# Weight blocks of 4 KB per partition and scan tables laid out by chunk and group, in a hybrid SSD and attention encoder

## The chip, the core and the metric

The kernel runs on one core of one Trainium2 chip. The time is device microseconds of one launch, as a median over runs. The core's engines run beside each other, each in its own order: TensorE (PE) for matrix products, VectorE (DVE), ScalarE (ACT) and GpSimd (POOL) for the rest, SyncE (SP), which here issues nearly all DMA transfers, and 16 DMA engines that carry them out.

## The reference

One layer over 512 tokens of width 1024, in float32. What is computed:

```
h    = rmsnorm(x) ;  z, xBC, dt, q, k, v, gates = split(h @ w_in)
y_s  = gated_rmsnorm(scan_forward(xBC, dt) + scan_backward(xBC, dt) + x*d_skip, z) @ w_ssd_out
y_a  = window_attention(q, k, v, sink, rel_bias) @ w_attn_out
x    = x + rmsnorm((sigmoid(g_s) * y_s + sigmoid(g_a) * y_a) @ w_o)
x    = x + rmsnorm(relu(rmsnorm(x) @ w_mlp_in)**2 @ w_mlp_out)
```

The scan works in 4 chunks of 128 tokens, in both directions, for 8 groups of 4 heads. Within a chunk the decay between tokens l and s is exp(cs[l] − cs[s]), where cs is the cumulative sum of dt·a over the chunk:

```
cb     = einsum('bclgn,bcsgn->bcgls', c, b)
y_diag = einsum('bcgls,bcgrls,bcsgrp->bclgrp', cb, decay, xdt)
y_off  = einsum('bclgn,bcgrpn,bcgrl->bclgrp', c, prev, exp(a_cs))
```

## The kernel before, in words

**Products.** Each product with a weight runs over blocks of 128 output columns and 1024 input channels. `cm` (L551) makes one "quantum" of each: its block is a tile wr of 128 partitions × 1024 floats (8 pieces of 128 channels), loaded by one DMA of 512 KB (`chunk_raw`, L478). A float32 product is made of three passes on rounded parts: ACT casts the block to wh (L498), POOL subtracts to wl (L502), in four pieces, and `mm3` (L429, with the matmul itself on L423) multiplies wh and wl with the activations' two parts into a bank pp. The activations' parts are made by `split` (L440 ACT for the rounded part, L441 DVE for the rest). In DRAM w_in, w_attn_out, w_ssd_out and w_mlp_in lie row by row, so that a block's partition collects 8 runs of 128 floats, 512 bytes each.

**The scan.** For a group g the conv of the products x, B and C runs on DVE (`conv`, L982 to L986, with L992 and L993 for the silu; the tiles are called u, B, C). `dt_math` makes cs once and writes it and its exp to the DRAM tables csT and csE, 64 rows (direction, group, head) of 512 tokens. For each chunk of each group, `load` (L1129, L1135) fetches rf and rb, the rows of 4 heads copied to all 128 partitions, forward and backward, and E, the exp for two pairs of heads, one head on each half of the partitions. `prep` makes of them, on POOL (L1148), ACT (L1150 to L1155) and DVE (L1145, L1151, L1156, L1157), the masked decay matrix m; PE multiplies m with x. `outs` adds the part from the states, weighed with E (L1185, L1186, L1190, L1191). `rms` (L1198 to L1219) then makes the group's norm: squares summed on POOL (ssq), a matmul with ones (its operand's two parts are called sh and sl), a row of 512 sums written to DRAM (rrow), read back as a column (rcol), raised to −1/2 on POOL (L416, L418), written to DRAM (L1219) and read as a row copied to all partitions (rstd, L408). `finish` multiplies it into the outputs yT on DVE (L1229), four operations in a row.

**Attention** works on heads in between: scores (KH, Q), softmax (P, with L915 to L924), the transposes of P (L427) copied out as pT by ACT or DVE (L935).

**Order.** All is emitted quantum by quantum, and then `chain` (L522) hands a stretch of instructions to a Planner, which simulates the engines with its own costs (L233, among them bytes and a fixed time for a DMA) and due times (L266), chooses each engine's order and fixes it by dependencies. SP's order, and so the place of each DMA among the others, is chosen in the same way. A DMA on SP also waits for the one eight places before it on the queue to land.

Of the kernel before, what the change touches and what calls it, by code (L numbers as in the profile page):

```python
# [65 lines left out]
def packed(given):  # L66

    rows = lambda n: given[n].reshape(-1, 128)
    xt, wv = given["x"][0, :256].T.reshape(8, 128, 256), np.concatenate(
        [given["w_in"][0][:, c:c + n].reshape(8, 128, n) for c, n in ((C_V, 256), (C_DT, 64))], axis=2)  # L70
    pieces = lambda a, cuts: np.concatenate([a[k0:k1].transpose(1, 0, 2).reshape(-1) for k0, k1 in cuts])
    cv = np.concatenate([rows(n) for n in ("conv_w", "conv_b", "b_gate", "ssd_norm", "pre_mlp_norm")]).T
    row = np.concatenate([given[n].reshape(-1) for n in ("dt_bias", "a_log", "attn_sink", "d_skip")])
    bucket, far = buckets()
    bias = np.ascontiguousarray(given["rel_bias_table"][bucket].T)
    bias[:, far] = NEG
    first = np.concatenate([rows("pre_mix_norm").T, xt[0]], axis=1)
    return {"cv": np.ascontiguousarray(cv), "row": row, "bias": bias,
            "xt": np.concatenate([first.reshape(-1), pieces(xt, X_CHUNKS[1:])]), "wv": pieces(wv, V_CHUNKS)}


# [283 lines left out]
class Trunk:  # L365
    def __init__(self, ctx, tc, ins, out, dbg=None):
        self.tc, self.nc, self.out = tc, tc.nc, out
        self.__dict__.update({"d_" + k: v for k, v in ins.items()})
        self.d_w_in = ins["w_in"][0]
# [417 lines left out]
    def dt_math(self):  # L787
# [41 lines left out]
        def rows():  # L829
            px = self.bank("ps")  # L830
            for c in range(4):
                self.tr(px[:64, c * 128:(c + 1) * 128], self.cs[:, c, :])
            csr, cse = get("csr"), get("cse")
            nc.vector.tensor_copy(csr[:64], px[:64])
            nc.scalar.activation(cse[:64], px[:64], AF.Exp)
            self.csT = self.dp.tile([64, 512], F32, name="csT")
            self.csE = self.dp.tile([64, 512], F32, name="csE")
            nc.sync.dma_start(self.csT, csr[:64])
            nc.sync.dma_start(self.csE, cse[:64])
            put(csr, cse)  # L840
            self.show("dt", self.dt)
            self.show("cs", self.cs)
# [5 lines left out]
    def kv_quanta(self):  # L848
        nc = self.nc
        get = self.slots.get  # L850
        self.KH, self.KL = [], []

        def k_done(ps):
            for j in range(2):
                a = slice(j * 64, j * 64 + 64)
                b = slice(64 - j * 64, 128 - j * 64)
                KH, KL = get("KH", dtype=F32R), get("KL", dtype=F32R)
                nc.scalar.copy(KH[a], ps[a])
                nc.vector.tensor_tensor(KL[a], ps[a], KH[a].bitcast(F32), op=ALU.subtract)
# [6 lines left out]
        return [self.cm(self.d_w_in, C_K + 128 * i, hh, k_done) for i in range(2)]  # L866

    def backward(self, ap):

# [2 lines left out]
    def q_quantum(self, i):  # L872

        nc = self.nc

        blocks = lambda ap: ap.rearrange("p (n t) -> p n t", t=128)

        def done(ps):
            for u in range(2):
                a = slice(u * 64, u * 64 + 64)  # L880
                b = slice(64 - u * 64, 128 - u * 64)
                q = self.slots.get("Q", dtype=F32R)
                self.Q[2 * i + u] = q
# [4 lines left out]
        return self.cm(self.d_w_in, C_Q + 128 * i, lambda: self.h, done)  # L888

    def attn_bias(self, h):  # L890
        bt = self.bt[h] = self.slots.get("bt", (128, 384))
# [68 lines left out]
    def gate_quantum(self, m, dst):  # L960
# [5 lines left out]
        return self.cm(self.d_w_in, C_GS + m * 128, lambda: self.h, done)  # L966

    def attn_out_quantum(self, m):
        def done(ps):
# [3 lines left out]
                for hi, lo in self.at_:  # L973
                    self.slots.put(hi, lo)

        return self.cm(self.d_w_attn_out[0], m * 128, lambda: self.at_, done)


    def conv(self, u, ps, b):
# [16 lines left out]
    def ssd_quanta(self, g):  # L996
# [48 lines left out]
        def z_done(i):  # L1045
# [9 lines left out]
            return done  # L1055

        hh = lambda: self.h
        x, rest = [self.cm(self.d_w_in, C_X + 256 * g + 128 * i, hh, x_done(i)) for i in range(2)], [
            self.cm(self.d_w_in, C_B + 128 * g, hh, bc_done("B", 16 + g)),
            self.cm(self.d_w_in, C_C + 128 * g, hh, bc_done("C", 24 + g)),  # L1060
        ]
        z = [self.cm(self.d_w_in, C_Z + 256 * g + 128 * i, hh, z_done(i)) for i in range(2)]
        pool = {"x": x, "B": rest[:1], "C": rest[1:], "z": z}
        return [pool[k].pop(0) for k in ORDER]

    def ssd_steps(self, g):
# [57 lines left out]
        def load(c):  # L1124
            def run():
                ch[c]["r"] = get("rf"), get("rb")
                for d, r in enumerate(ch[c]["r"]):
                    base = self.csT[32 * d + 4 * g:32 * d + 4 * g + 4, c * 128:(c + 1) * 128]
                    nc.sync.dma_start(v4(r), bass.AP(tensor=base.tensor, offset=base.offset, ap=[[0, 128], [512, 4], [1, 128]]))  # L1129
                ch[c]["E"] = get("E", (128, 2, 2, 128))  # L1130
                for d in dirs[3 - c]:
                    base = self.csE[32 * d + 4 * g:32 * d + 4 * g + 4, c * 128:(c + 1) * 128]
                    for i in range(2):
                        src = bass.AP(tensor=base.tensor, offset=base.offset + i * 512, ap=[[0, 64], [1024, 2], [1, 128]])
                        nc.sync.dma_start(ch[c]["E"][i * 64:(i + 1) * 64, d], src)  # L1135
            return run

        def prep(c):
# [157 lines left out]

    def ssd_out_quanta(self):

        w = self.d_w_ssd_out[0]
        banks = []  # L1300

        def part(k0, k1, c, n):
            return w[k0 * 128:k1 * 128, c:c + n].rearrange("(k p) n -> p k n", p=128), k1 - k0, n, "p"

        def most(parts):
            ps = self.bank("pp")
# [5 lines left out]
        def rest(parts):  # L1312
            wh, wl = parts[0]
            for m, ps in enumerate(banks):
                c = slice(m * 128, (m + 1) * 128)
                for k in (14, 15):
                    self.mm3(ps, (wh[:, k - 14, c], wl[:, k - 14, c]), self.ys[k], False, k == 15)
                self.ssd_out_done(ps, m)

        return [Quantum([part(0, 8, m * 128, 128), part(8, 14, m * 128, 128)], most) for m in range(2)] + [  # L1320
            Quantum([part(14, 16, 0, 256)], rest)] + [
            self.cm(w, m * 128, lambda: self.ys, lambda ps, m=m: self.ssd_out_done(ps, m)) for m in range(2, 8)]

    def load_wo(self, j, k):
# [131 lines left out]
        return 8 * part + n // 2 + 4 * (n % 2)  # L1456

    def up_quantum(self, i):
        return self.cm(self.d_w_mlp_in[0], self.block(i) * 128, lambda: self.h2, lambda ps: self.up_done(ps, i))

    def up_halves(self, n):

        w = self.d_w_mlp_in[0]
        chunks = [(w[:, m * 128:(m + 1) * 128].rearrange("(k p) n -> p k n", p=128), 8, 128, "p")
                  for m in map(self.block, range(n))]
        held, banks = [], []

        def product(m, t2):
# [241 lines left out]
```

## Time and profile before

| | us |
|---|---|
| median of 3 runs | 1084.91 (1084.78 to 1085.91) |
| the profiled execution | 1087.15 |
| its span, first to last instruction | 1085.4 |
| PE busy in it | 1072.1 (99%) |
| DVE, ACT, POOL busy | 742.0, 641.8, 801.2 |
| mean granted PE clock | 0.998 |

The profile comes from one execution of its own, a little above the median. Times of rows are microseconds from the span's start. A row of the timeline gives start, length, engine, line, operation and "out<-in" by tile names (numbers left out), a count where like rows were joined, and in brackets the idle time of the engine before it and what ended that. SPq is SP's issue of a DMA, not its transfer; "us to landing" of a DMA is the time from issue to its data being there. PE matmuls overlap by pipelining.

### The profile page before, as it was taken

What the parts mean: (1) busy time and instruction counts of PE and PEld (TensorE: products, weight loads), DVE (VectorE), ACT (ScalarE), POOL (GpSimd) and SP (SyncE); (2) the same over time, 40 slices, a digit from 0 to 9 for tenths busy, and PEclk for the clock granted to TensorE, in tenths of its full rate; (3) what the DMA queues carried; (4) which work ended last, traced back from release to release, by engine and by line L of the source; (5) the groups of instructions that cost most, each with busy time, mean ns of one, the idle gap of its engine ahead of it and who ended that gap; (6) DMA issues with size and microseconds to landing.
All of it is one profiled execution on the core that took longest, in us unless ns stands there. A gap on an engine that the chain in (4) does not pass through costs nothing. (4 is left out here: it accounts for less than half of the span.)

```text
span 1085.4 us, 16598 instructions
## 1 busy us (share of the span) xinstructions
PE 1072.1 (99%) x5542; PEld 897.3 (83%) x5542; DVE 742.0 (68%) x1281; ACT 641.8 (59%) x1378; POOL 801.2 (74%) x986
## 2 busy tenths in 40 slices
PE   9999999999999999999999999999999999999997
PEld 7888888888888888888878888889888888888885
DVE  5777787787787787787788853435673583584698
ACT  7756786776686767676768632323554544444552
POOL 5846558558568798999999876511688898898994
PEclk9999999999999999999999999999999999999999
DMA  8434424533545636354554464524322422424232
GB/s 273 121 101 121 120 78 123 141 98 95 123 108 130 151 112 157 90 165 120 153 150 135 138 191 118 173 82 155 100 75 59 156 80 76 156 77 148 87 98 78
DMA packets 208181, 133.20 MB, mean 123 GB/s; under 512 B 9560, under 2 KB 190296, under 8 KB 208096
## 3 DMA queue, kind: packets, MB, share of 16 engines
q1 hardware_dynamic: 207808, 131.76, 43.0%
q8 instruction: 43, 0.70, 0.3%
q10 hardware_dynamic: 288, 0.39, 0.1%
q14 instruction: 42, 0.34, 0.1%
HBM read 127.63 MB, written 4.49 MB: 122 GB/s over the span
## 5 line engine op out<-in xcount | busy, mean ns | idle before, releaser
L502 POOL TENSOR_TENSOR wl<-wr,wh 128x256 fp32r<-128x256 f32 (+1 forms) x500 | 423.8, 877 | 137.1 <-ACT wh L498 131.2
L423 PE MATMUL pp<-h,wh 128*128 128x512 f32 (+1 forms) x1712 | 523.4, 387 | 0.0
L423 PEld LDWEIGHTS pp<-h,wh 128*128 128x128 f32 x1712 | 316.3, 188 | 62.3 <-issue 0.7
L423 PE MATMUL pp<-h,wl 128*128 128x512 f32 (+1 forms) x856 | 332.3, 388 | 0.0
L498 ACT CAST wh<-wr 128x1024 fp32r<-128x1024 f32 x131 | 136.4, 1042 | 140.1 <-PE pp L423 123.4
L423 PEld LDWEIGHTS pp<-h,wl 128*128 128x128 f32 x856 | 160.8, 188 | 32.5 <-issue 0.5
L1546 POOL TENSOR_TENSOR wl<-wd,wh 128x256 fp32r<-128x256 f32 x158 | 130.4, 862 | 12.0 <-ACT wh L1543 12.0
L1543 ACT CAST wh<-wd 128x512 fp32r<-128x512 f32 x82 | 47.3, 618 | 32.4 <-PE ps L423 16.2
L423 PE MATMUL ps<-wl,fh 128*128 128x512 f32 x164 | 63.9, 390 | 0.0
L423 PE MATMUL ps<-wh,fl 128*128 128x512 f32 x164 | 63.8, 389 | 0.0
L423 PE MATMUL ps<-wh,fh 128*128 128x512 f32 x164 | 63.8, 389 | 0.0
L1413 DVE SCALAR_TENSOR_TENSOR pp<-pp,r 128x512 f32<-128x512 f32 (+1 forms) x31 | 17.6, 568 | 65.0 <-ACT r L1410 64.9
L1154 ACT ACTIVATE n<-cb,tables 128x128 f32<-128x128 f32 x128 | 49.0, 390 | 16.0 <-DVE cb L1145 15.6
L1150 ACT ACTIVATE rf<-rf,tables 128x128 f32<-128x128 f32 x128 | 42.4, 392 | 14.2 <-DMA rf<-csT 14.2
L986 DVE SCALAR_TENSOR_TENSOR u<-pp,cv,u 128x510 f32<-128x510 f32 (+1 forms) x64 | 47.6, 744 | 4.5 <-ACT u L982 3.3
L423 PE MATMUL pp<-yh,wl 128*128 128x512 f32 x128 | 49.8, 390 | 0.0
L423 PE MATMUL pp<-yh,wh 128*128 128x512 f32 x128 | 49.7, 389 | 0.0
L423 PE MATMUL pp<-yl,wh 128*128 128x512 f32 x128 | 49.6, 389 | 0.0
L1155 ACT ACTIVATE m<-cb,tables 128x128 f32<-128x128 f32 x128 | 48.8, 388 | 0.3 <-DVE cb L1145 0.2
L1190 POOL TENSOR_TENSOR w<-w,E 128x256 f32<-128x256 f32 x48 | 37.9, 802 | 14.3 <-DVE w L1186 13.0
L1084 POOL TENSOR_TENSOR xd<-x,tables 128x256 f32<-128x256 f32 x48 | 33.0, 706 | 16.5 <-ACT x L1009 12.8
L918 ACT ACTIVATE P<-P,mx 128x384 f32<-128x384 f32 (+1 forms) x64 | 35.2, 552 | 15.1 <-DVE mx L915 14.9
(273 smaller groups left out, 2158.1 us busy)
## 6 DMA issues: line engine op xcount, KB each, us to landing
wr<-in_w_in SPq DMA_DIRECT2D x74, 512.0 KB, 4.0
wr<-in_w_mlp_in SPq DMA_DIRECT2D x32, 512.0 KB, 4.2
wd<-in_w_mlp_out SPq DMA_DIRECT2D x64, 256.0 KB, 5.5
rf<-csT SPq DMA_DIRECT2D x32, 256.0 KB, 4.7
rb<-csT SPq DMA_DIRECT2D x32, 256.0 KB, 3.3
wr<-in_w_ssd_out SPq DMA_DIRECT2D x14, 512.0 KB, 4.1
E<-csE SPq DMA_DIRECT2D x96, 64.0 KB, 4.1
x<-in_x SPq DMA_DIRECT2D x16, 256.0 KB, 5.5
```

The costliest lines, as they stand in the source:

```text
L423: self.nc.tensor.matmul(out, lhsT, rhs, start=start, stop=stop, skip_group_check=more)
L498: self.nc.scalar.copy(hi[:, :m], raw)
L502: engines[e].tensor_tensor(lo[:, c], raw[:, c], hi[:, c].bitcast(F32), op=ALU.subtract)
L918: nc.scalar.activation(p[:, :w], p[:, :w], AF.Exp, bias=mx[:, n:n + 1], accum_out=sm[:, n:n + 1])
L986: nc.vector.scalar_tensor_tensor(u[:, a:e], ps[:, a + d:e + d], self.wtap(t, b), u[:, a:e], op0=ALU.mult, op1=ALU.add)
L1084: nc.gpsimd.tensor_tensor(v4(xd[:, d * 256:(d + 1) * 256]), v4(xs(c)), by_dir(self.coef, c)[:, d].unsqueeze(2).to_broadcast([128, 4, 64]), ...
L1150: nc.scalar.activation(v4(rf)[:, h], v4(rf)[:, h], AF.Identity, bias=ncs[:, 0, h:h + 1])
L1154: nc.scalar.activation(v4(n)[:, h], cb[:, 0], AF.Copy, scale=dt[:, 0, h:h + 1])
L1155: nc.scalar.activation(v4(m)[:, h], cb[:, 1], AF.Copy, scale=dt[:, 1, h:h + 1])
L1190: nc.gpsimd.tensor_tensor(wc, wc, E[:, d], op=ALU.add)
L1543: nc.scalar.copy(hi, src)
L1546: (nc.vector if q == 512 else nc.gpsimd).tensor_tensor(lo[:, c], src[:, c], hi[:, c].bitcast(F32), op=ALU.subtract)
```

## The change

The host now lays the four weights out in blocks [column block, group of 8 channel pieces, 128 partitions, 8 pieces, 128 columns]; the columns for dt, which have an array of their own already, are left out of w_in's. So every partition's 8 × 128 floats of a block lie together, 4 KB. The first two column blocks of w_ssd_out are loaded in pieces of 8, 6 and 2 channel pieces as before, the last piece for both in one transfer. The tables csT and csE are laid out by chunk, direction and group (csE also by the half of the partitions), so that the 4 heads of rf or rb are one run of 2 KB instead of 4 of 512 bytes, and the pair of heads of E one run of 1 KB instead of two of 512 bytes. E's two directions, where both are needed, come in one transfer for each half of the partitions. csE is written in two transfers instead of one. Arrays that the kernel no longer reads aren't passed. The lines of the changed kernel stand 4 to 8 further down (L1129 is L1136, L1135 is L1140, L478 is L485, L408 is L415, L423 is L430).

```diff
+    blocks = lambda a: np.ascontiguousarray(a.reshape(-1, 8, 128, a.shape[1] // 128, 128).transpose(3, 0, 2, 1, 4))
+    w_in = given["w_in"][0]
+    mats = {"w_in": np.concatenate([w_in[:, :C_DT], w_in[:, C_Q:]], axis=1)}
+    mats.update({n: given[n][0] for n in ("w_attn_out", "w_ssd_out", "w_mlp_in")})
...
+    @staticmethod
+    def inside(base, offset, *dims):
+        return bass.AP(tensor=base.tensor, offset=base.offset + offset, ap=[list(d) for d in dims])
...
-        nk = w.shape[0] // 128
-        chunks = [(w[k0 * 128:(k0 + 8) * 128, c:c + 128].rearrange("(k p) n -> p k n", p=128), 8, 128, eng)
-                  for k0 in range(0, nk, 8)]
+        nk = w.shape[1] * 8
+        chunks = [(w[c // 128, k0 // 8], 8, 128, eng) for k0 in range(0, nk, 8)]
...
-            nc.sync.dma_start(self.csT, csr[:64])
-            nc.sync.dma_start(self.csE, cse[:64])
+            chunks = lambda a: a.rearrange("p (c t) -> p c t", c=4)
+            nc.sync.dma_start(self.inside(self.csT, 0, [128, 64], [8192, 4], [1, 128]), chunks(csr[:64]))
+            for i in range(2):
+                nc.sync.dma_start(self.inside(self.csE, 4096 * i, [128, 32], [8192, 4], [1, 128]), chunks(cse[i:64:2]))
...
-                    base = self.csT[32 * d + 4 * g:32 * d + 4 * g + 4, c * 128:(c + 1) * 128]
-                    nc.sync.dma_start(v4(r), bass.AP(tensor=base.tensor, offset=base.offset, ap=[[0, 128], [512, 4], [1, 128]]))
-                ch[c]["E"] = get("E", (128, 2, 2, 128))
-                for d in dirs[3 - c]:
-                    base = self.csE[32 * d + 4 * g:32 * d + 4 * g + 4, c * 128:(c + 1) * 128]
-                    for i in range(2):
-                        src = bass.AP(tensor=base.tensor, offset=base.offset + i * 512, ap=[[0, 64], [1024, 2], [1, 128]])
-                        nc.sync.dma_start(ch[c]["E"][i * 64:(i + 1) * 64, d], src)
+                    nc.sync.dma_start(r, self.inside(self.csT, 8192 * c + 4096 * d + 512 * g, [0, 128], [1, 512]))
+                E = ch[c]["E"] = get("E", (128, 2, 2, 128))
+                d0, nd = dirs[3 - c][0], len(dirs[3 - c])
+                for i in range(2):
+                    nc.sync.dma_start(E[i * 64:(i + 1) * 64, d0:d0 + nd].rearrange("p d j t -> p d (j t)"),
+                                      self.inside(self.csE, 8192 * c + 4096 * i + 2048 * d0 + 256 * g, [0, 64], [2048, nd], [1, 256]))
```

The planner sees fewer transfers and so orders some instructions otherwise. Three places matter below. The first is SP's queue about 355 us into the profiled execution, around the read of the row rstd_478. Before:

```order
L478 DMA wr_456_4355<-in_w_in 128x8x128
L1135 DMA E_497_4374<-csE_689 64x2x128 x4
L1135 DMA E_535_4742<-csE_689 64x2x128
L1129 DMA rf_495_4370<-csT_688 128x4x128
L1135 DMA E_535_4742<-csE_689 64x2x128 x3
L1219 DMA rrow2_4197<-rcol_444_4196 128x4
L478 DMA wr_463_4442<-in_w_in 128x8x128
L1129 DMA rb_506_4488<-csT_688 128x4x128
L1135 DMA E_507_4491<-csE_689 64x2x128 x2
L408 DMA rstd_478_4194<-rrow2_4197 128x512
```

The same place of the changed kernel:

```order
L485 DMA wr_456_4342<-in_w_in_b 128x1024
L1140 DMA E_497_4361<-csE_689 64x2x256 x2
L1140 DMA E_535_4727<-csE_689 64x2x256 x2
L1136 DMA rf_495_4357<-csT_688 128x512
L1225 DMA rrow2_4184<-rcol_444_4183 128x4
L485 DMA wr_463_4427<-in_w_in_b 128x1024
L1136 DMA rb_506_4473<-csT_688 128x512
L1140 DMA E_507_4476<-csE_689 64x256 x2
L415 DMA rstd_478_4181<-rrow2_4184 128x512
```

Four transfers of E fewer stand ahead of the write of rrow2; the rest keeps its order.

The second place is about 415 to 445 us: SP's queue around rstd_554 (wr_514, wr_519 and wr_524 are weight blocks), and DVE's work behind it. SP before:

```order
L478 DMA wr_514_5050<-in_w_in 128x8x128
L1129 DMA rf_570_5095<-csT_688 128x4x128
L1129 DMA rf_560_4978<-csT_688 128x4x128
L1219 DMA rrow3_4891<-rcol_502_4890 128x4
L478 DMA wr_519_5115<-in_w_in 128x8x128
L408 DMA rstd_554_4888<-rrow3_4891 128x512
L1135 DMA E_600_5350<-csE_689 64x2x128 x4
```

SP of the changed kernel:

```order
L485 DMA wr_514_5031<-in_w_in_b 128x1024
L1136 DMA rf_570_5076<-csT_688 128x512
L1225 DMA rrow3_4874<-rcol_502_4873 128x4
L1140 DMA E_600_5331<-csE_689 64x2x256
L1136 DMA rf_560_4961<-csT_688 128x512
L1140 DMA E_600_5331<-csE_689 64x2x256
L415 DMA rstd_554_4871<-rrow3_4874 128x512
L485 DMA wr_519_5096<-in_w_in_b 128x1024
```

The weight block wr_519 moves from ahead of rstd_554 to behind it, E_600 from behind it to ahead of it. DVE before, at the same time:

```order
L986 SCALAR_TENSOR_TENSOR u_565_5041<-pp_510_4987,cv_348,u_565_5041 128x510
L1151 TENSOR_TENSOR rf_560_4978<-rf_560_4978,rb_561_4979 128x512
L993 SCALAR_TENSOR_TENSOR u_565_5041<-th_566_5047,u_565_5041 128x512
L1186 TENSOR_TENSOR w_514_4589<-ps_513_5008,w_514_4589 128x512
L1156 TENSOR_TENSOR m_568_5063<-m_568_5063,n_569_5064 128x512
L1229 SCALAR_TENSOR_TENSOR yT_558_4972<-w_442_3898,cv_348,rstd_554_4888 128x256
L1229 SCALAR_TENSOR_TENSOR yT_558_4972<-w_444_3908,cv_348,rstd_554_4888 128x256
L1229 SCALAR_TENSOR_TENSOR yT_559_4975<-w_442_3898,cv_348,rstd_554_4888 128x256
L1229 SCALAR_TENSOR_TENSOR yT_559_4975<-w_444_3908,cv_348,rstd_554_4888 128x256
```

DVE of the changed kernel:

```order
L1157 TENSOR_TENSOR rf_560_4961<-rf_560_4961,rb_561_4962 128x512
L1235 SCALAR_TENSOR_TENSOR yT_558_4955<-w_442_3887,cv_348,rstd_554_4871 128x256
L1235 SCALAR_TENSOR_TENSOR yT_558_4955<-w_444_3897,cv_348,rstd_554_4871 128x256
L1235 SCALAR_TENSOR_TENSOR yT_559_4958<-w_442_3887,cv_348,rstd_554_4871 128x256
L1235 SCALAR_TENSOR_TENSOR yT_559_4958<-w_444_3897,cv_348,rstd_554_4871 128x256
L994 SCALAR_TENSOR_TENSOR u_565_5022<-pp_510_4968,cv_348,u_565_5022 128x510
L1151 TENSOR_TENSOR cb_573_5120<-ps_523_5118,cst_296 128x256
L1162 TENSOR_TENSOR m_568_5044<-m_568_5044,n_569_5045 128x512
L1001 SCALAR_TENSOR_TENSOR u_565_5022<-th_566_5028,u_565_5022 128x512
```

The last tap of u_565 and its closing product move from ahead of the four yT to behind them.

The third place is PE at about 440 us, where m_568 and m_574, the decay matrices of two chunks, are multiplied with x. Before:

```order
L423 MATMUL pp_529_5210<-h_14_101,wl_516_5053 128x512
L423 MATMUL pp_529_5210<-h_16_103,wh_515_5052 128x512
L423 MATMUL pp_529_5210<-h_17_104,wh_515_5052 128x512
...
L423 MATMUL pp_536_5297<-h_6_93,wl_521_5118 128x512
L423 MATMUL ps_532_5231<-m_568_5063,x_515_4597 64x128 x4
L423 MATMUL ps_532_5231<-m_574_5141,x_515_4597 64x128 x4
L427 MATMUL ps_540_5337<-ident_73,B_576_5172 128x128 x4
```

PE of the changed kernel:

```order
L430 MATMUL pp_529_5191<-h_14_101,wl_516_5034 128x512
L430 MATMUL ps_532_5212<-m_568_5044,x_515_4582 64x128 x4
L430 MATMUL ps_532_5212<-m_574_5122,x_515_4582 64x128 x4
L430 MATMUL pp_529_5191<-h_16_103,wh_515_5033 128x512
L430 MATMUL pp_529_5191<-h_17_104,wh_515_5033 128x512
```

The eight matmuls move ahead of twelve of 512 columns: the last six of pp_529 and the first six of pp_536.

More of the change, by code (lines that the diff above doesn't have):

```diff
@@ L76, in packed @@
     bias[:, far] = NEG
+    blocks = lambda a: np.ascontiguousarray(a.reshape(-1, 8, 128, a.shape[1] // 128, 128).transpose(3, 0, 2, 1, 4))
+    w_in = given["w_in"][0]
+    mats = {"w_in": np.concatenate([w_in[:, :C_DT], w_in[:, C_Q:]], axis=1)}
+    mats.update({n: given[n][0] for n in ("w_attn_out", "w_ssd_out", "w_mlp_in")})
     first = np.concatenate([rows("pre_mix_norm").T, xt[0]], axis=1)
[L78 removed]
+    return {**{n + "_b": blocks(a) for n, a in mats.items()}, "cv": np.ascontiguousarray(cv), "row": row, "bias": bias,
             "xt": np.concatenate([first.reshape(-1), pieces(xt, X_CHUNKS[1:])]), "wv": pieces(wv, V_CHUNKS)}
@@ L865, in kv_quanta @@
         hh = lambda: self.h
-        return [self.cm(self.d_w_in, C_K + 128 * i, hh, k_done) for i in range(2)]
+        return [self.cm(self.d_w_in_b, C_K - 64 + 128 * i, hh, k_done) for i in range(2)]
     def backward(self, ap):
@@ L1314, in rest @@
             for m, ps in enumerate(banks):
-                c = slice(m * 128, (m + 1) * 128)
                 for k in (14, 15):
-                    self.mm3(ps, (wh[:, k - 14, c], wl[:, k - 14, c]), self.ys[k], False, k == 15)
+                    self.mm3(ps, (wh[:, m, k * 128 - 1792:k * 128 - 1664], wl[:, m, k * 128 - 1792:k * 128 - 1664]),
+                             self.ys[k], False, k == 15)
                 self.ssd_out_done(ps, m)
-        return [Quantum([part(0, 8, m * 128, 128), part(8, 14, m * 128, 128)], most) for m in range(2)] + [
-            Quantum([part(14, 16, 0, 256)], rest)] + [
+        tail = w[0:2, 1, :, 6:8].rearrange("m p k n -> p m (k n)")
+        return [Quantum([(w[m, 0], 8, 128, "p"), (w[m, 1, :, :6], 6, 128, "p")], most) for m in range(2)] + [
+            Quantum([(tail, 2, 256, "p")], rest)] + [
             self.cm(w, m * 128, lambda: self.ys, lambda ps, m=m: self.ssd_out_done(ps, m)) for m in range(2, 8)]
@@ L1458, in up_quantum @@
     def up_quantum(self, i):
-        return self.cm(self.d_w_mlp_in[0], self.block(i) * 128, lambda: self.h2, lambda ps: self.up_done(ps, i))
+        return self.cm(self.d_w_mlp_in_b, self.block(i) * 128, lambda: self.h2, lambda ps: self.up_done(ps, i))
     def up_halves(self, n):
-        w = self.d_w_mlp_in[0]
-        chunks = [(w[:, m * 128:(m + 1) * 128].rearrange("(k p) n -> p k n", p=128), 8, 128, "p")
-                  for m in map(self.block, range(n))]
+        w = self.d_w_mlp_in_b
+        chunks = [(w[m, 0], 8, 128, "p") for m in map(self.block, range(n))]
         held, banks = [], []
```

22 lines of the change are left out of this document (10 added, 12 removed).

## The prediction

> **What bounds the kernel now.** I read the busy line of the page first, then the busy time in stretches, then the places where TensorE (PE) waits. The first row is the page's; the others are stretches with their length, then busy time and count of PE, weight load, DVE, ACT and POOL, then PE's clock, DMA share and GB/s.
>
> ```profile
> PE 1072.1 (99%) x5542; PEld 897.3 (83%) x5542; DVE 742.0 (68%) x1281; ACT 641.8 (59%) x1378; POOL 801.2 (74%) x986
> ```
> ```profile
> 0.00:20.00 20.00, 17.94 (x77) 13.45 (x78) 11.43 (x31) 12.94 (x28) 8.67 (x17) 1.00 0.96 311
> 20.00:210.00 190.00, 190.00 (x1106) 162.60 (x1105) 141.74 (x315) 134.51 (x310) 121.36 (x159) 1.00 0.45 118
> 210.00:420.00 210.00, 207.36 (x1222) 174.45 (x1221) 163.83 (x303) 148.41 (x359) 153.02 (x191) 1.00 0.47 118
> 420.00:580.00 160.00, 159.07 (x837) 132.15 (x836) 125.44 (x180) 117.50 (x268) 147.61 (x179) 1.00 0.51 138
> ...
> 1075.00:1085.40 10.40, 2.71 (x12) 1.90 (x11) 6.15 (x11) 1.45 (x4) 1.52 (x2) 0.81 0.41 151
> ```
>
> PE is busy for 1072.1 of 1085.4 us. Of the 13.3 us without it, 20.00 − 17.94 = 2.06 lie in the start and 10.40 − 2.71 = 7.69 in the tail, and no edit touches either: the start loads x and the columns of v, the tail holds no changed load. What is left is 210.00 − 207.36 = 2.64 and 160.00 − 159.07 = 0.93, together **3.57 us**. As the matmuls stay the same in number and shape, this is all that the change can win. The rows of PE with a wait in brackets, behind it what ended it:
>
> ```profile
> 240.60 1.09 PE L423 MATMUL ps<-m,x 128*64 128x128 f32 x16 [0.21 <-DVE pT L935]
> ```
> ```profile
> 258.32 0.44 PE L423 MATMUL ps<-KH,Q 128*128 128x384 f32 x1 [0.94 <-ACT pT L935]
> ```
> ```profile
> 287.69 0.88 PE L427 MATMUL ps<-ident,P 128*128 128x128 f32 x5 [0.52 <-DVE P L924]
> ```
> ```profile
> 383.23 0.66 PE L423 MATMUL ps<-m,x 128*64 128x128 f32 x8 [0.97 <-DVE m L1157]
> ```
> ```profile
> 569.02 0.50 PE L423 MATMUL ps<-sh,ones_r 128*128 128x512 f32 x1 [0.93 <-ACT sh L440]
> ```
>
> They add up to 0.21 + 0.94 + 0.52 + 0.97 + 0.93 = 3.57, so these five are the whole of it. None is a wait for a weight. The waits of the other engines and of the DMA queue (total, times, longest) say why:
>
> ```profile
> POOL wl L502 <- ACT wh L498: 131.2, 67, 8.9
> ACT wh L498 <- PE pp L423: 123.4, 45, 4.4
> ```
> ```profile
> SPq L478 <- POOL wl L502: 282.3, 107, 8.4
> ```
>
> The queue's weight issues (L478) wait 282.3 us for buffers that the split frees, and the split waits for PE. Weights are paced by PE, not PE by weights. Where nothing holds it, PE runs at one pace, as a piece of the chain that ended last shows (start, us, count):
>
> ```profile
> 616.99 118.59 PE pp L423 x523
> ```
>
> 118.59 / 523 = 0.227 us a matmul of 512 columns.
>
> **The change part by part.** *Weight blocks.* Issue rows (KB, median us to landing) and two stretches of traffic, the first with 512-byte packets only, the second mostly of 2 KB:
>
> ```profile
> wr<-in_w_in SPq DMA_DIRECT2D x74, 512.0 KB, 4.0
> ...
> rf<-csT SPq DMA_DIRECT2D x32, 256.0 KB, 4.7
> rb<-csT SPq DMA_DIRECT2D x32, 256.0 KB, 3.3
> ...
> rstd<-rrow SPq DMA_DIRECT2D x8, 256.0 KB, 5.3
> ...
> rrow<-rcol SPq DMA_DIRECT2D x8, 2.0 KB, 2.8
> ```
> ```profile
> DMA packets 982, 0.50 MB, mean 248 GB/s; under 512 B 15, under 2 KB 982, under 8 KB 982
> ...
> q1 hardware_dynamic: 982, 0.50, 87.5%
> ```
> ```profile
> DMA packets 1039, 1.78 MB, mean 297 GB/s; under 512 B 106, under 2 KB 190, under 8 KB 1039
> ...
> q1 hardware_dynamic: 1039, 1.78, 93.4%
> ```
>
> The first lasts 2.0 us: 2.0 × 16 × 0.875 / 982 = 28.5 ns a packet, so a block of 1024 takes 1024 × 28.5 / 16 = 1.8 us. Per second of queue time it moves 248 / 0.875 = 283 GB/s, the second 297 / 0.934 = 318. At that rate 512 KB take 1.6 us; 4-KB packets are not in the trace. Bounds for a block: 0 saved (as now) to 0.9 (half). I take 0.3. Over some 128 blocks this is 40 us of queue time, and it is **worth nothing by itself**, hidden by the buffer waits above; the pieces of w_ssd_out with 3 KB and 1 KB runs too, since PE doesn't idle between 580 and 1075 us. A block counts only where something urgent is queued behind it.
>
> The Trainium skill, DMA: Bandwidth & Descriptors, section Specifications, puts the smallest transfer for line rate at 512 B. By it the packets of before lose nothing and the new layout gives nothing at all, which is the second rival below; the trace agrees to 318 / 283 = 1.12.
>
> *Tables.* rf and rb go from 512 packets of 512 B to 128 of 2 KB. The row nearest in form is rstd: also 2 KB of one row to each of 128 partitions, and it takes 5.3 us to land against 4.7 and 3.3. That doesn't promise a faster table; I bound it between 0.6 us slower (5.3 − 4.7) and 0.5 faster (half of 512 × 28.5 / 16 = 0.9) and take no gain for one alone. E goes from 96 to 64 transfers:
>
> ```profile
> L1135 SPq DMA_DIRECT2D E<-csE x96: 573/597/2304, 80.7 to 573.0; - x96
> ```
>
> 32 × 0.597 = 19 us of SP's issue time go; as SP waits over 280 us, this too counts only at a place. The one more write of csE stands long before the first read at 80.7 us: nothing.
>
> *Where something urgent is queued.* Both waits that a scan's load leads to start at rstd, the row that yT waits for on DVE (L1229); behind it in DVE's order stand m and P. DVE's wait at the first place; then POOL's pow, SP's rows and DVE's wait at the second:
>
> ```profile
> 283.98 0.48 DVE L1229 SCALAR_TENSOR_TENSOR yT<-w,cv,rstd 128x256 f32<-128x256 f32 x1 [1.97 <-DMA rstd<-rrow]
> ```
> ```profile
> 360.14 1.02 POOL L418 TENSOR_TENSOR rcol<-rcol,mhalf 128x4 f32<-128x4 f32 x1
> ```
> ```profile
> 361.28 0.54 SPq L1219 DMA_DIRECT2D rrow<-rcol  x1
> 361.93 0.38 SPq L478 DMA_DIRECT2D wr<-in_w_in  x1
> 362.41 0.52 SPq L1129 DMA_DIRECT2D rb<-csT  x1
> ...
> 364.44 0.46 SPq L408 DMA_DIRECT2D rstd<-rrow  x1
> ```
> ```profile
> 371.21 1.36 DVE L1229 SCALAR_TENSOR_TENSOR yT<-w,cv,rstd 128x256 f32<-128x256 f32 x2 [4.79 <-DMA rstd<-rrow]
> ```
>
> 383.23: four E issues fewer ahead would give SP 2.4 us, but the write of rrow must wait for POOL's pow, which ends at 360.14 + 1.02 = 361.16, and rstd for that write to land (2.8): 361.28 + 2.8 = 364.1. So rstd is issued when it was. It lands 6.7 us later, against 5.3 in the median, behind the packets of wr and rb; wr gives 0.3 to 0.9, rb −0.6 to 0.5, the E traffic a little. With 1.0 us it would be at the median's 5.7. From yT to m DVE works through its row nearly without a gap, so what rstd gains PE gains, up to 0.97. Ends 0 and 0.97; I take **0.6**.
>
> 287.69: rb and rf (1024 packets, 1.8 us) stand directly ahead of rstd. The same bounds for two tables, −1.2 to +1.0 us, against 0.52 that are needed; a gain ends at 0.52, a loss is paid in full. I take **0.2** (ends −1.2 and 0.52).
>
> *Order.* 240.60: two matmuls of 0.227 us now stand ahead of m,x, so the wait of 0.21 for pT is filled: **0.2** (ends 0 and 0.21). 258.32: the cast of pT on ACT stands behind xh; one small operation of ACT moves out from ahead of it. No row prices that; I take **0.2** (ends 0 and 0.94), near the lower end, since a cast of a weight block still stands there. 569.02: the rms matmul waits for sh, and sh for ssq on POOL; a table operation moves from ahead of ssq to behind it:
>
> ```profile
> 557.84 1.22 POOL L1148 TENSOR_TENSOR rb<-rb,tables 128x512 f32<-128x512 f32 x1
> ```
>
> sh comes up to 1.22 us earlier, but the matmul on sl now follows that on sh at once, and sl is DVE's difference, which comes after sh. I take **0.3** (ends 0 and 0.93).
>
> *New waits.* Two places of PE get work earlier. Rows of DVE, PE and SP there, and the page's group of conv taps (busy, mean ns):
>
> ```profile
> 430.60 3.22 DVE L1229 SCALAR_TENSOR_TENSOR yT<-w,cv,rstd 128x256 f32<-128x256 f32 x4 [0.30 <-DMA rstd<-rrow]
> ...
> 441.80 1.15 DVE L1157 TENSOR_TENSOR m<-m,rf 128x512 f32<-128x512 f32 x1
> ```
> ```profile
> L986 DVE SCALAR_TENSOR_TENSOR u<-pp,cv,u 128x510 f32<-128x510 f32 (+1 forms) x64 | 47.6, 744 | 4.5 <-ACT u L982 3.3
> ```
> ```profile
> 434.31 0.82 PE L427 MATMUL ps<-ident,u 128*128 128x128 f32 x6
> ```
> ```profile
> 421.41 0.33 SPq L1219 DMA_DIRECT2D rrow<-rcol  x1
> 424.53 0.37 SPq L478 DMA_DIRECT2D wr<-in_w_in  x1
> 425.00 0.53 SPq L408 DMA_DIRECT2D rstd<-rrow  x1
> ```
>
> On DVE the last tap of u_565 now stands behind the four yT and so behind rstd. If rstd lands as before, yT ends at 430.60 + 3.22 = 433.8; four operations at the tap's 0.744 (tap, cb, m, u's product) make u ready at 436.8, where PE wants it at 434.31: a wait of 2.5. But rstd moves ahead of the weight load wr_519: it can be issued at 421.41 + 2.8 = 424.2 instead of 425.00, without 1.8 us of packets just ahead of it. 0.8 + 1.8 give up to 2.6 less what E and rf ahead of it cost; at 2.2, u is ready at 434.6. I take **+0.3** (ends 0 and 2.5). The product with m_574 stands 12 matmuls earlier, 12 × 0.227 = 2.7 us; m_574 was ready at 441.80 + 1.15 = 442.95 and PE did not wait for it, so it would be up to 2.7 late, unless its table (queued behind yT) comes that much sooner, as it does if rstd does; on DVE it also moves ahead of some of B's taps. I take **0** (ends 0 and 2.7). The two don't add up: a wait for u puts off the need for m_574.
>
> *Sum.* −0.6 − 0.2 − 0.2 − 0.2 − 0.3 + 0.3 = **−1.2**, against the profiled execution of 1087.15 us (span 1085.4, 1.75 outside it): 1085.95 for such an execution. That execution is 2.24 us above the median of 1084.91; the difference is carried over as it is: **1083.7**. A measurement of this kernel can tell about 0.2%, 2.2 us, from no change: the forecast is within that.
>
> **The rivals.** *All five go, nothing new.* 3.57 us: 1081.3. For it: each needs 1 us or less. Against it: 258.32 and 569.02 hang on orders that no transfer moves far. Chance 0.17.
>
> *The tables come no sooner* (rstd's 5.3 us to landing speaks for it). Then 287.69 and 383.23 stay, and only order helps: −0.7 + 0.3 = −0.4, 1084.5. If the packets did not grow as the diff says, it would be the same. Chance 0.24. The rule of the Trainium skill quoted above would come out here.
>
> *Slower.* rstd_554 lands no earlier than now, because the E and rf that stand ahead of it take the place of wr_519. Then PE waits 2.5 for u at 434, or 2.7 in all with m_574 at 441, and nothing else is won but the 0.2 at 240: +2.5, 1087.4. It begins to cost where rstd lands less than 2.2 us earlier than its 430.6, and is paid in full if it lands there or later. Against it: one E and one table are less than a weight block. Chance 0.14.
>
> **How the numbers follow.** Forecast 0.45, the others 0.17, 0.24 and 0.14. The range goes from the first rival, 1081.3, over the second to 1086.5, which takes in the 1.2 us that 287 may lose and half of a new wait, and leaves out the full price of the last rival and little else. Faster by over 0.2% is below 1082.7: the first rival, and 0.15 of the forecast's 0.45, since the ends of its terms reach there: 0.32. Slower by over 0.2% is above 1087.1: of the last rival 0.11. Within: 0.57.
>
> **What would show it.** Packets of weights fall to an eighth, those of rf and rb to a quarter, and E issues to 64, with PE's busy time still 1072 us: the edits do what they say, and cost nothing. PE's waits in 210 to 580 us are then 2.4 instead of 3.57: the wait at 383 is down to 0.4 and DVE's wait for rstd there below 4.2; around 287 it is shorter than 0.5. If rstd still takes 6.7 us, the second rival holds. A wait of PE for u or m between 430 and 445 shows the third. I am wrong in kind if PE's busy time moves by over 1 us, or if the start or tail changes.

## The result, and the profile after

The changed kernel took 1082.94 us in the median of 11 runs (1082.44 to 1083.88), the kernel before 1086.14 beside it (1084.71 to 1089.1): a ratio of **0.9972, 95% interval 0.9963 to 0.9981**. On another chip the same pair gave 0.9986 (0.9977 to 0.9994), 1083.43 against 1084.92. So it is faster, by 1.5 to 3.2 us. The forecast was 1083.7, worked out from the median of 1084.91 that was shown first, and a change within 0.2% was held the likeliest: the second pair of runs lies within it, the first a little beyond.

The profiled execution took 1082.52 us with a span of 1080.6. The busy line of its page, the stretches that answer to those of before (length, then busy time and count of PE, weight load, DVE, ACT, POOL, PE's clock, DMA share, GB/s), and the one wait of PE left between 20 and 1071 us:

```profile
PE 1071.3 (99%) x5542; PEld 898.3 (83%) x5542; DVE 744.5 (69%) x1281; ACT 640.1 (59%) x1378; POOL 801.5 (74%) x986
```
```profile
0.00:20.00 20.00, 18.54 (x82) 14.36 (x83) 12.14 (x33) 13.67 (x30) 8.65 (x17) 1.00 0.93 333
20.00:210.00 190.00, 190.00 (x1105) 162.44 (x1104) 142.68 (x314) 134.44 (x313) 120.50 (x158) 1.00 0.38 116
210.00:420.00 210.00, 209.74 (x1246) 176.97 (x1245) 167.29 (x306) 151.14 (x364) 159.69 (x198) 1.00 0.42 121
420.00:580.00 160.00, 160.00 (x850) 133.83 (x849) 126.07 (x184) 116.76 (x267) 147.12 (x177) 1.00 0.46 139
...
1071.00:1080.60 9.60, 2.05 (x10) 1.35 (x8) 5.51 (x11) 1.45 (x4) 1.52 (x2) 0.71 0.38 143
```
```profile
216.78 0.52 PE L434 MATMUL ps<-ident,P 128*128 128x128 f32 x3 [0.26 <-DVE P L932]
```

All five waits of before are gone and one small new one has come: 0.26 us instead of 3.57. The two spans differ by 4.8 us: 3.31 by these waits, 0.60 in the start (18.54 − 17.94), 0.14 in the tail (7.69 − 7.55), and 0.75 in PE's modelled busy time. The start can't be put down to the change: PE's busy time in it was 18.54 and 17.37 in two profiles of the changed kernel, 17.94 and 17.35 in two of the kernel before. The transfers did what the diff says:

```profile
DMA packets 61380, 133.19 MB, mean 123 GB/s; under 512 B 9064, under 2 KB 18792, under 8 KB 61296
```
```profile
wr<-in_w_in_b SPq DMA_DIRECT2D x74, 512.0 KB, 3.6
...
rf<-csT SPq DMA_DIRECT2D x32, 256.0 KB, 3.9
rb<-csT SPq DMA_DIRECT2D x32, 256.0 KB, 5.2
```

There are 61,380 packets instead of 208,181 for the same 133 MB; a weight block lands in 3.6 us instead of 4.0, rf in 3.9 instead of 4.7, while rb's median is longer (5.2 against 3.3). These medians rest on few: the trace of before tells the landing of one rb alone (3.3 at the least, in the middle and at the most) and of two rstd (3.9 and 6.7). At the place around 371 us of before, SP's rows and DVE's wait for rstd now read:

```profile
357.66 0.33 SPq L1225 DMA_DIRECT2D rrow<-rcol  x1
358.38 0.33 SPq L485 DMA_DIRECT2D wr<-in_w_in_b  x1
358.82 0.64 SPq L1136 DMA_DIRECT2D rb<-csT  x1
...
360.90 0.38 SPq L415 DMA_DIRECT2D rstd<-rrow  x1
```
```profile
366.34 1.91 DVE L1235 SCALAR_TENSOR_TENSOR yT<-w,cv,rstd 128x256 f32<-128x256 f32 x2 [2.13 <-DMA rstd<-rrow]
```

From rstd's issue to the work on it: 366.34 − 360.90 = 5.4 us, 371.21 − 364.44 = 6.8 before. DVE's wait fell from 4.79 to 2.13.

### The profile page after: what moved, and what is told of

Same layout as the page of the kernel before. It is cut to its first block, busy times and chain, and to the rows that moved or that the text cites. A ratio compares the mean times of both kernels' runs of the same rounds, so it can differ in the third digit from the quotient of the medians.

```text
span 1080.6 us, 16563 instructions
## 1 busy us (share of the span) xinstructions
PE 1071.3 (99%) x5542; PEld 898.3 (83%) x5542; DVE 744.5 (69%) x1281; ACT 640.1 (59%) x1378; POOL 801.5 (74%) x986
## 2 busy tenths in 40 slices
DMA packets 61380, 133.19 MB, mean 123 GB/s; under 512 B 9064, under 2 KB 18792, under 8 KB 61296
## 4 chain that ended last, share of the span: by engine, by line
PE 97%; DVE 1%; DMA 1%; issue 0%; ACT 0%; SPq 0%; POOL 0%; DVEq 0%; POOLq 0%
PE pp L430 70%; PE ps L430 24%; PE ps L434 3%; DMA wr<-in_wv 1%; DVE P L932 0%; SPq L670 0%; DVE wl L600 0%; DVEq L1710 0%; DVE ag L1623 0%; PE pp L434 0%; POOLq L1710 0%; ACT wh L597 0%; ACT x L740 0%; DVE acc L1601 0%; DVE m L1163 0%
## 5 line engine op out<-in xcount | busy, mean ns | idle before, releaser
L430 PE MATMUL pp<-h,wh 128*128 128x512 f32 (+1 forms) x1712 | 524.5, 388 | 0.0
L430 PEld LDWEIGHTS pp<-h,wh 128*128 128x128 f32 x1712 | 316.3, 188 | 62.4 <-issue 1.2
L430 PE MATMUL pp<-h,wl 128*128 128x512 f32 (+1 forms) x856 | 332.0, 388 | 0.0
L430 PEld LDWEIGHTS pp<-h,wl 128*128 128x128 f32 x856 | 160.9, 188 | 32.2 <-issue 0.2
L430 PE MATMUL ps<-wl,fh 128*128 128x512 f32 x164 | 64.0, 390 | 0.0
L430 PE MATMUL ps<-wh,fl 128*128 128x512 f32 x164 | 63.9, 390 | 0.0
L430 PE MATMUL ps<-wh,fh 128*128 128x512 f32 x164 | 63.9, 389 | 0.0
L430 PE MATMUL pp<-yh,wl 128*128 128x512 f32 x128 | 49.8, 390 | 0.0
L430 PE MATMUL pp<-yh,wh 128*128 128x512 f32 x128 | 49.7, 389 | 0.0
L430 PE MATMUL pp<-yl,wh 128*128 128x512 f32 x128 | 49.7, 389 | 0.0
```

Source lines behind the costliest of these rows:

```text
L430: self.nc.tensor.matmul(out, lhsT, rhs, start=start, stop=stop, skip_group_check=more)
```

## The experiments

Two theories. **O, order:** E's merged transfers make the planner choose another order, and that is what makes the kernel faster. **T, transfers:** the scan's loads (rf, rb, rstd) are ready sooner, because they are shorter themselves or meet shorter packets of weights. They can be taken apart: with E's 96 transfers kept, every engine's order was row for row that of before, whatever the layouts; with E merged it was that of the changed kernel.

| run | layouts that are new | order | ratio to before, 95% | PE's waits, 20 to 580 us |
|---|---|---|---|---|
| e1 | weights | before | 0.9989 (0.9976 to 1.0001) | 0.37 |
| e2 | weights, rf and rb | before | 0.9983 (0.9972 to 0.9995) | 0.25 |
| e3 | E | changed | 1.0009 (0.9996 to 1.0022) | 3.08 |
| e4 | E, rf and rb | changed | 0.9989 (0.9979 to 0.9999) | 0.92 |
| e10 | rf and rb | before | 0.9983 (0.9974 to 0.9992) | 0.00 |
| e8 | all (the changed kernel) | changed | 0.9986 (0.9977 to 0.9994) | 0.26 |

The waits are stretch length less PE's busy time, from one profile each. The kernel before had 3.57 in one profile and 2.31 in another (e12). The ratios of e1 to e4 were taken on one chip, those of e5 to e8 on a second, of e9 to e11 on a third, each beside the kernel before; their intervals reach some 0.001 to either side, so differences of 0.0005 say nothing.

**e1, the weights alone.** The diff's lines for csT, csE, rf, rb and E left out:

```diff
-            nc.sync.dma_start(self.inside(self.csT, 0, [128, 64], [8192, 4], [1, 128]), chunks(csr[:64]))
+            nc.sync.dma_start(self.csT, csr[:64])
...
-                    nc.sync.dma_start(r, self.inside(self.csT, 8192 * c + 4096 * d + 512 * g, [0, 128], [1, 512]))
+                    nc.sync.dma_start(v4(r), bass.AP(tensor=base.tensor, offset=base.offset, ap=[[0, 128], [512, 4], [1, 128]]))
```

> Only the weights in blocks of 4 KB; the tables and their 96 transfers of E as before, and with them every engine's order as before. Theory O (the gain is the new order, which the merged transfers of E bring about): all five waits of PE stay, the time is that of before within 0.5 us, ratio 0.9995 to 1.0005. Theory T (the gain is data that lands sooner, above all rstd behind shorter packets): the waits at 383 and 288 us shrink by 0.3 to 0.9 us together, ratio 0.9990 to 0.9997.

Measured 0.9989, with an interval that just touches 1. Its stretches say more than the ratio:

```profile
210.00:420.00 210.00, 209.69 (x1236) 176.61 (x1234) 164.51 (x304) 150.88 (x364) 155.46 (x195) 1.00 0.42 121
420.00:580.00 160.00, 159.94 (x861) 133.50 (x861) 126.71 (x184) 118.15 (x270) 148.12 (x180) 1.00 0.46 140
```

0.31 + 0.06 = 0.37 us of waits, in the order of before. The waits can go without the new order, against theory O, and T took too little: those at 258 and 569 us went as well. What is left is 0.32 for a pT at 293 us, a new place.

**e2, all layouts but E's, in the order of before.**

```diff
-            for i in range(2):
-                nc.sync.dma_start(self.inside(self.csE, 4096 * i, [128, 32], [8192, 4], [1, 128]), chunks(cse[i:64:2]))
+            nc.sync.dma_start(self.csE, cse[:64])
```

(and E's loads as before)

> Weights in blocks and rf and rb as one run of 2 KB, but E in 96 transfers from the old table, so that every engine's order is that of before. Theory O: ratio 0.9995 to 1.0005, the five waits stay. Theory T: nearly the whole gain, 2 to 3 us, ratio 0.9972 to 0.9982; by the prediction's own terms for transfers, 0.8 us, 0.9993.

0.9983: a gain like the changed kernel's (0.9972 and 0.9986) without its order.

**e3, E merged alone.** Only the lines of csE and E from the change.

> Only E's table and its 64 transfers are new; weights, rf and rb keep their 512-byte packets. Every engine's order is that of the changed kernel. Theory O: nearly the whole gain, 2.5 to 3.2 us, ratio 0.9970 to 0.9977, and no wait of PE over 0.3 us after the start. Theory T: the waits at 383 and 288 us stay, and new ones may come at 434 to 441 us where the new order needs rstd sooner; ratio 0.999 to 1.002.

1.0009, no gain. PE's waits of over 1 us, in the new order with the old packets:

```profile
381.87 0.66 PE L427 MATMUL ps<-m,x 128*64 128x128 f32 x8 [1.51 <-DVE m L1162]
```
```profile
434.32 0.98 PE L431 MATMUL ps<-ident,u 128*128 128x128 f32 x7 [1.31 <-DVE u L999]
```

The first is the wait at 383 of before, and larger; the second is the new wait for u_565 behind the four yT. The only other is 0.26 for a P at 217. At 240, 258, 288 and 569 us PE does not wait in this profile: with the old packets, too, the new order can do without these four waits, but it pays for them at the other places, and nothing is won. The order that E's merging brings needs rstd sooner, and with the old packets it isn't there.

**e4, both tables, weights as before.** e3 with rf and rb as one run of 2 KB.

> Both tables new (rf and rb as 2 KB, E merged), the weights row by row as before; order of the changed kernel. Theory O: as the changed kernel, ratio 0.9970 to 0.9977. Theory T: between, 0.9985 to 0.9995, since the weight packets ahead of rstd are still 512 bytes.

0.9989, waits 0.92: with rf and rb in 2 KB, 2.2 us of e3's waits are gone. The longest that is left is for sl, which the prediction had named as the limit of what the new order can win at 569:

```profile
566.50 0.50 PE L427 MATMUL ps<-sl,ones_r 128*128 128x512 f32 x1 [0.52 <-DVE sl L445]
```

**e5 and e6, packet size with the block's place held.** Each block of w_in and w_attn_out is one 512-KB piece of DRAM, but laid out so that a transfer has Q runs for each partition: Q = 8 gives 512 bytes, Q = 16 gives 256 (Q stands below for the number). Tables and order as before; w_mlp_in and w_ssd_out stay in blocks of 4 KB, which e7 below shows to be worth nothing.

```diff
+    runs = lambda a: np.ascontiguousarray(blocks(a).reshape(-1, a.shape[0] // 1024, 128, Q, 1024 // Q).transpose(0, 1, 3, 2, 4))
...
+        if src.shape[0] == Q:
+            self.nc.sync.dma_start(raw.rearrange("p (q n) -> p q n", q=Q), src.rearrange("q p n -> p q n"))
+            return
```

> As the run with the weights alone (tables and order of before), but each block of w_in and w_attn_out lies in its 512 KB of DRAM in such an order that a transfer still has 1024 runs of 512 bytes. It tells packet size from the block's lying in one piece. Theory P (fewer, longer packets get out of the way of the scan's loads sooner): as before, ratio 0.9995 to 1.0008, the five waits are there, rb at 231 us of the unchanged timing is late again. Theory C (one piece of DRAM): as the weights alone, 0.9980 to 0.9992.

1.0004 (0.9995 to 1.0013), waits 1.27 + 0.44 = 1.71 us: no gain in time from the block's lying in one piece. But theory P's five waits came only in part. PE waits at 287, 382 and 567 us, and neither at 240 nor at 258; and POOL finds rb there, where the kernel before waits 1.22 us for it (shown under e10):

```profile
229.60 1.04 POOL L1158 TENSOR_TENSOR rb<-rb,tables 128x512 f32<-128x512 f32 x1
```

So at this one place something else about the old weights than the size of their packets kept rb; what it is stays open.

> The same with 2048 runs of 256 bytes a block of w_in and w_attn_out: the suspected cost is doubled. Theory P, if a packet of 256 bytes takes near as long as one of 512 (27 ns): the tables and rstd land 1 to 2 us later, PE's waits grow from 3.6 to 6 to 12 us, ratio 1.002 to 1.008. Theory C: 0.9980 to 0.9992. If only bytes count: as before.

1.0103 (1.0089 to 1.0117), some 11 us slower and beyond the 1.008 that was expected. PE's longest wait, and the stretches around its two worst places:

```profile
289.14 0.44 PE L435 MATMUL ps<-ident,P 128*128 128x128 f32 x2 [3.34 <-DVE P L934]
```
```profile
289.00:294.00 5.00, 4.50 (x15) 3.55 (x16) 4.87 (x10) 3.34 (x11) 2.46 (x3) 0.66 0.51 112
...
386.00:389.00 3.00, 0.66 (x8) 0.45 (x8) 2.90 (x3) 3.00 (x8) 2.68 (x3) 0.97 0.09 22
389.00:396.00 7.00, 6.71 (x22) 5.17 (x23) 6.73 (x11) 3.02 (x6) 5.18 (x8) 0.52 0.87 182
```

PE waits at three of the places of before, for longer (3.34 at 289, 1.52 at 389, 1.20 at 579), and once more just ahead of the second (1.72 at 387). At 240 and 258 it doesn't wait, as in e5. The waits are 7.02 + 1.30 = 8.3 us in all, inside the 6 to 12 that were expected. That is 4.7 of the 9.7 us by which the span is longer than that of before. The rest is PE's busy time, 1077.3 us for the same matmuls against 1072.1: its clock falls in two stretches, and 5 × (1 − 0.66) + 7 × (1 − 0.52) = 5.1 us. Twice the packets cost far more than a quarter of them brings (e9).

**e9, runs of 2 KB** (Q = 2).

> As the weights alone, with 256 runs of 2 KB a block of w_in and w_attn_out. Theory P: a 2-KB run moves bytes about as fast as a 4-KB one, so the gain is that of the weights alone: 0.9980 to 0.9996, with less than 1 us of PE's waits left between 20 and 1070 us. If it is the number of packets that counts, half-way between: 2 us of waits left.

0.9991 (0.9982 to 1.0000), waits 0.08 us. 2 KB does what 4 KB does (0.9989 in e1); between 512 bytes and 2 KB lies the step. The traces show it also in the waits of the other engines for the scan's loads. Before, then e9:

```profile
DVE yT L1229 <- DMA rstd<-rrow: 15.9, 5, 7.6
ACT rf L1150 <- DMA rf<-csT: 14.2, 10, 2.4
POOL rb L1148 <- DMA rb<-csT: 9.8, 8, 2.6
```
```profile
ACT rf L1160 <- DMA rf<-csT: 10.7, 10, 2.0
DVE yT L1239 <- DMA rstd<-rrow: 9.3, 3, 5.8
POOL rb L1158 <- DMA rb<-csT: 4.7, 5, 2.1
```

The same three rows, summed, in the runs with the tables and the order of before (e7, below, is the run whose early weights are as before and whose late ones are in blocks):

| early weights | waits for rstd, rf and rb, us | DMA queue busy, 20 to 580 us |
|---|---|---|
| rows, 512 bytes (before, e12, e7) | 39.9, 36.5, 33.1 | 46.8%, 46.7%, 46.7% |
| blocks, 256 bytes (e6) | 49.7 | 54.3% |
| blocks, 512 bytes (e5) | 33.7 | 46.3% |
| blocks, 2 KB (e9) | 24.7 | 42.4% |
| blocks, 4 KB (e1) | 26.0 | 41.2% |

Equal bytes in fewer packets keep the queue busy for less time, and loads that the weights' edit doesn't touch are waited for less.

The Trainium skill, DMA: Bandwidth & Descriptors, section Specifications, names 512 B as the smallest transfer at line rate. In this case's traces 512-byte packets still moved less per second of queue time than mostly 2-KB ones (283 against 318 GB/s, as the prediction works out), and with the step to 2 KB 9.0 us of waits for the scan's loads went (33.7 − 24.7). That sentence is about bandwidth and leaves out what a bulk load's packets do to a small load beside it.

**e7, a control: only w_mlp_in and w_ssd_out in blocks.**

```diff
-    mats.update({n: given[n][0] for n in ("w_attn_out", "w_ssd_out", "w_mlp_in")})
+    mats = {n: given[n][0] for n in ("w_ssd_out", "w_mlp_in")}
```

> Only w_mlp_in and w_ssd_out in blocks of 4 KB; w_in, w_attn_out, tables and order as before. After 580 us, where most of these blocks are loaded, PE does not wait for anything. Theory P: nothing gained, ratio 0.9993 to 1.0005, with PE's five waits between 240 and 570 us still there, 3 us or more in all. A rival, that shorter DMA time helps PE or DVE everywhere: 0.9985 to 0.9995, with these waits unchanged and PE's busy time smaller.

1.0001 (0.9993 to 1.0010). The blocks loaded where PE never waits are worth nothing, as the prediction had it. PE's waits were 1.71 us, less than expected.

**e10, rf and rb alone.** Two transfers a chunk as one run of 2 KB, csT laid out for it, the rest as before.

> Only csT's layout and rf and rb as one run of 2 KB; weights, E and order as before. The prediction took no gain for one table alone and 0.2 us at 288: ratio 0.9993 to 1.0005. If a table that lands sooner is worth what the weights' packets were worth to it: 0.9982 to 0.9993, with rb at 231 us of the unchanged timing ready about 1 us sooner and the wait at 258 gone.

0.9983, and no wait of PE at all between 20 and 580 us:

```profile
210.00:420.00 210.00, 210.00 (x1247) 177.03 (x1245) 166.12 (x306) 152.10 (x365) 158.35 (x198) 1.00 0.45 121
420.00:580.00 160.00, 160.00 (x852) 133.63 (x851) 124.70 (x185) 118.12 (x272) 146.64 (x178) 1.00 0.53 140
```

The smallest edit of all has a gain that can't be told from the changed kernel's. Where it starts can be seen at 231 us. SP's issues in before, then POOL's work on that rb in before and in e10:

```profile
224.82 0.37 SPq L1129 DMA_DIRECT2D rb<-csT  x1
225.42 0.37 SPq L478 DMA_DIRECT2D wr<-in_w_in  x1
```
```profile
230.86 1.04 POOL L1148 TENSOR_TENSOR rb<-rb,tables 128x512 f32<-128x512 f32 x1 [1.22 <-DMA rb<-csT]
```
```profile
229.44 1.04 POOL L1152 TENSOR_TENSOR rb<-rb,tables 128x512 f32<-128x512 f32 x1
```

rb is issued 0.6 us **ahead** of a weight block, and still POOL waits 1.22 us for it. In e10 it is there when POOL is. As the orders are the same, row can be set against row: ahead of this one e10 runs 0.16 us ahead of before, from it on 1.43 on POOL, and DVE and ACT carry that lead on, through rf, m, C's conv and sl, to pT at 258. In e1 the lead comes at the same row (−1.00 after +0.23), though there rb is as before and only the weight blocks have changed.

That this row is the root of the wait at 258 is borne out by all nine profiles with the order of before. POOL waits for this rb in three of them, before, e12 and e7 (1.22, 0.55 and 0.93 us), and in these three alone PE waits at 258 (0.94, 0.55 and 0.91). The rows of e7:

```profile
230.31 1.04 POOL L1157 TENSOR_TENSOR rb<-rb,tables 128x512 f32<-128x512 f32 x1 [0.93 <-DMA rb<-csT]
```
```profile
257.79 0.44 PE L428 MATMUL ps<-KH,Q 128*128 128x384 f32 x1 [0.91 <-ACT pT L944]
```

The three are those whose w_in lies row by row and whose rb has 512-byte runs. Either edit, w_in in blocks or the tables in 2-KB runs, is enough here; in e5 and e6 the blocks are, without longer packets.

**e11, the planner told of faster transfers.** The changed kernel with one constant:

```diff
-RATE, EARLY, LAND = 260, 350, 2500
+RATE, EARLY, LAND = 320, 350, 2500
```

> The changed kernel with the planner's bytes per ns raised from 260 to 320, near what long runs reach; only the order of a few dozen instructions changes. One wait of 0.3 us is left to win between 20 and 1070 us, so at best 0.4 us over the changed kernel: 0.9963 to 0.9990 against before; a wait of over 0.5 us in the new places would show as 0.999 and more.

0.9993 (0.9984 to 1.0002), with 1.37 us of waits: not better than the changed kernel. Its new waits are at the two places that the prediction named:

```profile
432.27 0.87 PE L434 MATMUL ps<-ident,u 128*128 128x128 f32 x6 [0.58 <-DVE u L1001]
```
```profile
439.96 0.66 PE L430 MATMUL ps<-m,x 128*64 128x128 f32 x8 [0.57 <-DVE m L1163]
```

**e12, before profiled a second time.** e5 and e7 had shown fewer waits than the first profile of before.

> The kernel before, as it is, for a second profile. The two runs whose early weights and tables are as in before (blocks in 512-byte runs, late weights only) had 1.7 us of waits of PE between 20 and 580 us, where the profile of before had 3.6. Theory S (that execution was a heavy one; the waits differ from one to the next): about 1.7 us, a span near 1083.5. If the edits of those two runs were worth 1.9 us after all: 3.4 to 3.7 us of waits, in the five places, and a span near 1085.4.

Span 1084.0, and four waits, between the two expectations:

```profile
257.50 0.44 PE L423 MATMUL ps<-KH,Q 128*128 128x384 f32 x1 [0.55 <-ACT pT L935]
```
```profile
287.05 0.87 PE L427 MATMUL ps<-ident,P 128*128 128x128 f32 x5 [0.71 <-DVE P L924]
```
```profile
381.95 0.66 PE L423 MATMUL ps<-m,x 128*64 128x128 f32 x8 [0.33 <-DVE m L1157]
```
```profile
567.55 0.50 PE L423 MATMUL ps<-sh,ones_r 128*128 128x512 f32 x1 [0.72 <-ACT sh L440]
```

0.55 + 0.71 + 0.33 + 0.72 = 2.31 us where the first had 3.57. The size of these waits differs from one execution to the next; their places hardly do.

## Why the prediction was right or wrong

*The bound* held. The waits of PE between 210 and 580 us were all that could be won, and nearly all of them went: the first rival's trace (chance 0.17), not the forecast's, which had 2.4 us of waits left. Late weights are worth nothing: shown by e7.

*The sum* of −1.2 lies near the second chip's 1.5 and short of the first's 3.2. That it came so near is luck in part, as two errors worked against each other. Each term took a part of its wait where the whole went (the total without new waits was −1.5 of 3.57). And the waits themselves were taken from a heavy execution: with the 2.31 us of the second profile less 0.26 the trace gives 2.05, inside the two measurements. To carry the difference of 2.24 us to the median over "as it is" was wrong in kind: part of it was made of the very waits that the terms were shares of (the second profile's execution, at 1085.75, had 1.26 us of them less).

*The step that failed* is the one on tables, "take no gain for one alone". It priced rf and rb by rstd's median to landing, 5.3 us against 4.7 and 3.3, figures that hold whatever stood in the queue with each, the 3.3 of a single rb and the 5.3 of two rstd. e10 shows the two tables alone, without the rest of the change, to be worth 0.9983, and POOL's waits for rb to fall to 4.0 us, from 9.8 and 7.5 in the two profiles of before. With it falls "258.32 and 569.02 hang on orders that no transfer moves far", and "a block counts only where something urgent is queued behind it": the rb at 231 us is queued ahead of the block, and changing the blocks alone (e1) made it come in time. The prediction followed the wait at 258 back to ACT's order and stopped there; its root was POOL's wait for rb 27 us earlier, in a row whose bracket named the DMA. For 569, e1 and e10 show only that it goes in the order of before; which of the loads ahead of it counted was not separated. Nor is it known why rb is late at 231 with w_in in rows, and not in e5 and e6.

*Order*, −0.7 with 0.3 against it: the three terms were right in kind, the whole was not. In e3, with the new order and the old packets, the waits at 240, 258 and 569 are gone, and that at 288 too (240 says little, as e5, e7 and e12 lack it in the old order); but 1.51 us at 383 and 1.31 at 434 stand against them (0.3 had been taken), and e3 is not faster. With the new layouts the order is not needed: e2 and e10 have the gain without it.

*383 us:* The working has rstd land at "the median's 5.7" after its issue; the median that it quotes is 5.3, and 5.7 is 6.7 − 1.0. Measured are 5.4 in the changed kernel and 5.7 in e10. But "rstd is issued when it was" was wrong. It is issued 364.44 − 360.90 = 3.5 us earlier in the changed kernel. In e10, where the orders are the same, PE runs 2.36 us ahead of before just ahead of this place, and rstd is issued 364.44 − 361.30 = 3.1 us earlier: POOL's pow ahead of it had gained too. From issue to use it takes 1.1 less: DVE starts 367.00 − 361.30 = 5.7 us after the issue, 6.8 before.

*434 and 441 us:* the third rival's mechanism is real. With rstd behind the old packets PE waits 1.31 us for u (e3; 2.5 had been priced). In the changed kernel DVE starts the four yT at 423.74 without a wait, against 430.60, and PE waits at neither place.

*The new wait* of 0.26 at 217 us was not foreseen. It stands in every run with the new order (0.26 in e3, e4 and both profiles of the changed kernel) and is the one trace that the order left in the changed kernel.

## What to carry to other kernels

When an engine that is 99% busy waits for another, follow the row back past the engine's own order to the first bracket that names a DMA, however many microseconds earlier: here a lead of 1.43 us on POOL was still 1.38 on ACT 27 us later. Price a small urgent load by its place among the transfers that are in flight with it, those issued just behind it as well, not by the median of its kind. And take a second profile before sharing out waits of a microsecond: here they were 2.3 us in one execution and 3.6 in another.

## What the runs showed of the hardware

PE's clock: in the run with 256-byte packets PE stood 3.34 us and, some 100 us later, 1.72 and 1.52 us close together; the granted clock was 0.66 over the 5 us from the end of the first on and 0.52 over 7 us that begin within the last. In the other profiles, with no wait over 1.6 us between 20 and 580 us, it was 1.00 throughout that part. The Trainium skill, TensorE: Matmul & The Clock Gate, Part 1, describes such a gate, with a window of some 3.4 us; the first of these waits agrees with it in length. In the second case the clock fell with no single wait as long, but with 1.72 and 1.52 us of waiting only 0.66 us of work apart.

Packets: for weights that share the DMA engines with urgent loads, the step between slow and fast lies between 512 bytes and 2 KB (1.0004 and 0.9991; 33.7 and 24.7 us of waits for these loads), and one step down, to 256 bytes, costs 1.0%, in part by PE's clock.
